# Encoder trunk: the first pair's up-projection weights prepared during the output projection, and a written order for three engines

## The chip, the cores and the metric

The kernel runs on one core of one Trainium2 chip. The metric is the device time of one launch in microseconds (us), as the median of the runs. Engines are named as in the profile: PE is TensorE's matmul, DVE is VectorE, ACT is ScalarE, POOL is GpSimd, and SP issues the DMAs.

## The reference

Two layers, each a mixing part and a gated MLP, on 1024 tokens of 1024 channels, all in float32:

```python
for l in range(DEPTH):
    h = _rmsnorm(x, norm1_g[l])
    ...
    x = x + mix @ w_out[l]

    h2 = _rmsnorm(x, norm2_g[l])
    up = _dwconv3(h2 @ ffn_w_up[l], ffn_conv_w[l])
    gate, val = jnp.split(up, 2, axis=-1)
    x = x + (jax.nn.silu(gate) * val) @ ffn_w_down[l]
```

`ffn_w_up` has 1024 rows and 5632 columns: 22 tiles of 128 columns for the gate and 22 for the value.

## The kernel before, in words

Every float32 product is made of three matmuls in the type fp32r. An operand is split into a high part (a copy to fp32r, on ACT, line 108) and a low part (operand minus high part, on DVE or POOL, line 119); the product is high·high + high·low + low·high (`block_mm`, line 768).

The up projection is done by a scheme with seven products of blocks instead of eight. The activations are cut into four blocks of channels by tokens, the weights of one tile pair (gate tile f, value tile 22 + f) into `b11`, `b21`, `b12`, `b22`. Sums and differences of blocks are the operands. Of the weights these are 11, 21, 22 and the differences T1 to T4, formed in place one after the other by POOL (`up_prep`, line 745); of the activations 11, 12, 22 and the sums S1 to S4. Each tile f takes seven products of 12 matmuls, 84 in all: 11·11, 12·21, S1·T1, S2·T2, S3·T3, S4·22 and 22·T4.

The stage around the change, in both layers:

- `out_proj(b, 1)` is the second half of the output projection for each of eight token blocks b: five splits of the mixing output (ACT and POOL), 24 matmuls on PE, a residual add on DVE (line 661).
- `norm_a` takes the sum of squares on ACT (line 227), the scale 1/sqrt on POOL (lines 123 and 127) and multiplies on DVE (line 229).
- `norm2_b` transposes on PE (line 679), then makes the activation blocks: a split into 11 and 12 for the first four token blocks and into 22 for the last four. For these last four it also forms S3 and S2 on DVE (lines 695 and 696), and S1 and S4 on POOL (lines 697 and 698), in place in two buffers, H2 (S1, S4) and H3 (S3, S2).
- `norm2_end` splits S1 to S4, 1024 columns at a time, ACT high and DVE (or POOL) low.
- `up_ahead` makes 11·11 and 12·21 of tiles 0 and 1 early, since these need no sums (four products, 48 matmuls). `up_prep` forms and splits the rest of the weights. `up_tile` makes the remaining products. Its copies u1 and p5 go to the buffer H3, which becomes free only when S2 and S3 have been split. S3·T3 is summed onto the PSUM bank of S2·T2, so it begins only when u1 has been copied away (line 797).

Nothing in this stage has an order written by hand: the framework's scheduler sets the order of each engine's queue (only the attention's PE queue is written by hand). Each engine then runs its queue strictly in that order.

The lines of the trace: 768 the products, 679 the transposes, 119 and 108 the splits, 745 the weight differences, 695 to 698 the sums, 796 and 797 the adds and copies of `up_tile`.

Of the kernel before, what the change touches and what calls it, by code (L numbers as in the profile page):

```python
# [43 lines left out]
UPRING = ("E0", "E1", "E2", "E5", "E6", "E7", "E9", "G6", "G7")  # L44
# [11 lines left out]
CWE = ("p", "p")  # L56


class Trunk:
# [640 lines left out]
    def norm2_end(self):  # L700

        r0, r1 = self.raw
        for n, src, where, els in (
            ("S1", r0[:, 0:4], self.xo[1], "vv"),
            ("S2", r1[:, 4:8], ("W1", "W4", "Z0", "Z1"), "vv"),
            ("S3", r1[:, 0:4], ("G0", "G2", "G3", "W2"), "vv"),
            ("S4", r0[:, 4:8], ("W5", "G4", "G1", "G5"), "vp"),
        ):
            if isinstance(where, str):
                t = self.A[n] = self.slot(where, [2, 4, 512], F32R)  # L710
                for k in (0, 2):
                    self.split(t[:, 0, k : k + 2], t[:, 1, k : k + 2], src[:, k : k + 2], "a", els[k // 2])
            else:
                t = self.A[n] = [self.S(w, [2, 512], F32R) for w in where]
                for k in range(2):
                    self.split(t[k], t[2 + k], src[:, 2 * k : 2 * k + 2], "a", els[k])

    def a_op(self, n, k):
# [5 lines left out]
    def up_load(self, L, f):  # L724
        raws = []
        for j, m in enumerate((f, NFF + f)):
# [11 lines left out]

    def up_prep(self, f, raws, B):


        b11, b21, b12, b22 = raws

        def sub(out, a, b):
            self.nc.gpsimd.tensor_tensor(out=out, in0=a, in1=b, op=ALU.subtract)  # L745

        if not B:
            B["11"] = self.up_split(b11, "v")
        sub(b11, b12, b11)
        B["T1"] = self.up_split(b11)  # L750
        sub(b11, b22, b11)
        B["T2"] = self.up_split(b11, "v")
        if "21" not in B:
            B["21"] = self.up_split(b21)
        sub(b12, b22, b12)
        B["T3"] = self.up_split(b12, "v")
        B["22"] = self.up_split(b22)
        sub(b21, b21, b11)
        B["T4"] = self.up_split(b21)
# [13 lines left out]
    def up_ahead(self, f, raws):  # L773

        B = {"11": self.up_split(raws[0], "v"), "21": self.up_split(raws[1], "v")}
        u, c2 = self.acc("pa"), self.acc(("po", "pf")[f])
        self.block_mm(u, "11", B["11"], True, False)
        self.block_mm(c2, "12", B["21"], True, True)
        if f == 0:
# [3 lines left out]
        return B, u, c2, p1  # L783

    def up_tile(self, f, B, ahead=None):
# [160 lines left out]
    def run(self, depth):  # L946
# [6 lines left out]
        for L in range(depth):  # L953
# [61 lines left out]
            for b in range(NB + 2):  # L1015
                if b < NB:
                    self.out_proj(b, 1)
                    nc.sync.dma_start(xout[b], self.x[b])
                if 0 <= b - 1 < NB:
                    xs[b - 1] = self.norm_a(b - 1, self.x[b - 1], g2, ("G1", "G5"))  # L1020
                if 0 <= b - 2 < NB:
                    self.norm2_b(b - 2, xs[b - 2])
                if b - 2 in (5, 6):
                    f = len(ahead)
                    raws[f] = self.up_load(L, f)
                    ahead.append(self.up_ahead(f, raws[f]))
            self.norm2_end()
            B = {0: ahead[0][0], 1: ahead[1][0]}
            self.up_prep(0, raws[0], B[0])
            for f in range(NFF):  # L1030
                if f + 1 < NFF:
                    if f + 1 >= 2:
                        raws[f + 1], B[f + 1] = self.up_load(L, f + 1), {}
                    self.up_prep(f + 1, raws.pop(f + 1), B[f + 1])
                self.up_tile(f, B.pop(f), ahead[f][1:] if f < 2 else None)
# [65 lines left out]
```

## Time and profile before

| what | value |
|---|---|
| median of three runs | 2300.79 us (2300.1 to 2304.73) |
| profiled execution, its own time | 2304.89 us |
| its span | 2303.1 us |
| PE busy | 2222.9 us (97%) |
| DVE, ACT, POOL busy | 1657.6, 1121.1, 1287.6 us |

The profiled execution is one run; its span is the time from its first to its last instruction, 1.8 us less than its own time. Times in the trace count from the start of the span. The second half of the output projection of layer 0 ends on PE at about 490 us, that of layer 1 at about 1632 us.

### The profile page before, as it was taken

How to read it: one execution, taken by the hardware profiler on the slowest of the kernel's cores; microseconds unless marked ns; L12 is line 12 of the kernel's file. 1: busy time of each engine (PE TensorE's matmuls, PEld its weight loads, DVE VectorE, ACT ScalarE, POOL GpSimd, SP SyncE). 2: the span in 40 equal slices, each digit the busy share in tenths (PEclk: the TensorE clock that was granted, in tenths of full speed). 3: DMA queues.
4: the chain of work that ended last, by engine and by line, in shares of the span. 5: the costliest groups of instructions: out<-in, count | busy, mean ns of one | idle time of the engine just before them, and what ended most of it. 6: DMA issues, size and time to landing. Idle time of an engine off the chain costs nothing.

```text
span 2303.1 us, 29303 instructions
## 1 busy us (share of the span) xinstructions
PE 2222.9 (97%) x10564; PEld 1840.9 (80%) x10564; DVE 1657.6 (72%) x2123; ACT 1121.1 (49%) x2009; POOL 1287.6 (56%) x1133
## 2 busy tenths in 40 slices
PE   7999999989999999799999999999899999988998
PEld 6887887868888888588878878878688888876887
DVE  5468887276777777988645688862767777779885
ACT  4246776354544444443242467754545444444431
POOL 5463335685555554776454533356765555556761
PEclk9999999999999999899999999999899999999999
DMA  5000003222232325843230000041223333357431
GB/s 183 23 28 10 10 10 95 98 83 87 92 115 92 115 92 175 304 156 106 67 122 6 28 10 10 10 163 48 74 87 101 110 105 105 105 190 268 152 96 74
DMA packets 166852, 218.97 MB, mean 95 GB/s; under 512 B 11799, under 2 KB 117811, under 8 KB 166707
## 3 DMA queue, kind: packets, MB, share of 16 engines
q1 hardware_dynamic: 166706, 217.10, 28.3%
q8 instruction: 83, 1.36, 0.2%
q14 instruction: 63, 0.51, 0.1%
HBM read 159.92 MB, written 57.15 MB: 94 GB/s over the span
## 4 chain that ended last, share of the span: by engine, by line
PE 89%; DVE 4%; POOL 2%; DMA 2%; ACT 1%; issue 1%; SPq 0%; DVEq 0%; POOLq 0%; ACTq 0%
PE pa L768 20%; PE big L920 10%; PE pf L768 9%; PE pf L266 5%; PE po L768 5%; PE pa L536 5%; PE pa L920 3%; PE pa L134 3%; PE pa L133 3%; PE big L520 3%; PE big L519 3%; PE pa L132 3%; PE po L548 2%; PE po L549 2%; PE pf L920 2%; PE po L920 2%
## 5 line engine op out<-in xcount | busy, mean ns | idle before, releaser
L528 POOL TENSOR_SCALAR H<-H,rv 128x1024 f32<-128x1024 f32 x128 | 144.8, 1131 | 272.2 <-DVE rv L527 272.2
L119 POOL TENSOR_TENSOR E<-E,E 128x512 fp32r<-128x512 f32 (+1 forms) x123 | 167.6, 1364 | 172.7 <-ACT E L108 172.2
L108 ACT ACTIVATE E<-E 128x512 fp32r<-128x512 f32 (+1 forms) x227 | 141.6, 629 | 182.0 <-POOL E L745 69.3
L768 PE MATMUL pa<-H,E 128*128 128x512 f32 x840 | 210.8, 395 | 12.3 <-DVE H L796 12.3
L541 DVE TENSOR_TENSOR E<-pa,E 128x512 fp32r<-128x512 f32 x256 | 173.4, 688 | 49.6 <-ACT E L540 48.2
L768 PEld LDWEIGHTS pa<-H,E 128*128 128x128 f32 x840 | 160.0, 191 | 46.7 <-DVE H L796 13.2
L540 ACT ACTIVATE E<-pa 128x512 fp32r<-128x512 f32 x256 | 152.9, 597 | 90.4 <-PE pa L536 89.2
L536 PEld LDWEIGHTS pa<-ident,H 128*128 128x128 f32 x1024 | 128.0, 141 | 42.8 <-issue 5.1
L536 PE MATMUL pa<-ident,H 128*128 128x128 f32 x1024 | 154.9, 274 | 6.6 <-DVE E L541 6.6
L522 DVE TENSOR_REDUCE nm<-big 128x1 f32<-128x1024 f32 x128 | 155.7, 1216 | 6.7 <-PE big L520 6.6
L353 DVE SCALAR_TENSOR_TENSOR big<-H,cst,big 128x1023 f32<-128x1023 f32 x44 | 56.6, 1287 | 143.8 <-ACT big L352 143.8
L797 ACT ACTIVATE H<-pa 128x512 f32<-128x512 f32 x128 | 76.0, 594 | 164.0 <-PE pa L768 148.0
L525 ACT ACTIVATE H<-big,nm 128x1024 f32<-128x1024 f32 x128 | 142.4, 1112 | 17.7 <-DVE nm L522 17.6
L119 DVE TENSOR_TENSOR E<-E,E 128x512 fp32r<-128x512 f32 (+1 forms) x109 | 117.9, 1084 | 24.1 <-ACT E L108 24.1
L266 PE MATMUL pf<-H,G 128*128 128x512 f32 x320 | 130.7, 429 | 2.7 <-DVE Z L394 2.7
L768 PE MATMUL pa<-W,E 128*128 128x512 f32 x340 | 119.2, 400 | 12.7 <-ACT W L108 12.7
L108 ACT ACTIVATE G<-E 128x512 fp32r<-128x512 f32 (+2 forms) x126 | 68.6, 556 | 106.1 <-PE pa L133 21.0
L745 POOL TENSOR_TENSOR E<-E 128x512 f32<-128x512 f32 x66 | 103.1, 1563 | 4.4
L768 PE MATMUL po<-H,E 128*128 128x512 f32 x408 | 104.6, 389 | 0.0
L548 PE MATMUL po<-E,E 128*128 128x512 f32 x256 | 101.5, 396 | 2.1 <-DVE E L564 2.1
L108 ACT ACTIVATE G<-H 128x512 fp32r<-128x512 f32 (+1 forms) x94 | 58.5, 649 | 90.7 <-PE big L920 43.7
L549 PE MATMUL po<-E,E 128*128 128x512 f32 x256 | 101.3, 396 | 0.0
(430 smaller groups left out, 6554.1 us busy)
## 6 DMA issues: line engine op xcount, KB each, us to landing
E<-in_ffn_w_up_dram SPq DMA_DIRECT2D x66, 512.0 KB
gdram<-H SPq DMA_DIRECT2D x66, 512.0 KB
H<-gdram SPq DMA_DIRECT2D x66, 512.0 KB
out_dram<-H SPq DMA_DIRECT2D x32, 512.0 KB
E<-in_w_in_dram SPq DMA_DIRECT2D x30, 512.0 KB
H<-out_dram SPq DMA_DIRECT2D x24, 512.0 KB
H<-in_ffn_w_down_dram SPq DMA_DIRECT2D x24, 512.0 KB
W<-in_ffn_w_up_dram SPq DMA_DIRECT2D x22, 512.0 KB
```

Source lines behind the costliest of these rows:

```text
L108: nc.scalar.activation(out, in_, AF.Copy)
L119: e.tensor_tensor(out=l, in0=src, in1=h.bitcast(F32), op=ALU.subtract)
L266: mm(acc, a[:, k, :], b, start=k + j == 0, stop=k == KC - 1 and j == 2)
L522: nc.vector.tensor_reduce(out=nm, in_=S, op=ALU.max, axis=AX.X, negate=True)
L528: nc.gpsimd.tensor_scalar(out=p, in0=p, scalar1=rv, scalar2=1.0, op0=ALU.mult, op1=ALU.mult)
L536: nc.tensor.transpose(pt[:, r * P : (r + 1) * P], pu[:, r, kc * P : (kc + 1) * P], self.ident)
L540: nc.scalar.activation(hl[:, 0, :], pt, AF.Copy)
L541: nc.vector.tensor_tensor(out=hl[:, 1, :], in0=pt, in1=hl[:, 0, :].bitcast(F32), op=ALU.subtract)
L548: self.nc.tensor.matmul(O, v, hl[:, 0, :], start=kc == 0, stop=False)
L549: self.nc.tensor.matmul(O, v, hl[:, 1, :], start=False, stop=kc == 7)
L768: mm(out, w, x, start=first and k + j == 0, stop=k == 3 and j == 2, skip_group_check=True,)
L920: nc.tensor.matmul(o, p, r, start=n + q == 0 and (m % 2 == 1 or m == 0), stop=n == len(ops) - 1 and q == 2, skip_group_check=True,)
```

## The change

Three things are changed. The weights of tile 0 and half of those of tile 1 are loaded in the program at block 2, and tile 0's 11, 21 and T1 are split, and all its differences formed, at block 4, during the output projection. After the last block of the output projection DVE, POOL and ACT follow the order in which the program is written (`manual_schedule`), up to the end of the preparation of tile 1; in it S2 is split before S1 and S3, and S4 later, with both low parts on DVE. In `up_tile` the first two tiles do S2·T2 before S1·T1. PE's order is still the scheduler's.

```diff
+MANUAL = {mybir.EngineType.DVE, mybir.EngineType.Pool, mybir.EngineType.Activation}
...
-    def norm2_end(self):
+    def norm2_end(self, names):
...
         for n, src, where, els in (
+            ("S2", r1[:, 4:8], ("W1", "W4", "Z0", "Z1"), "vv"),
             ("S1", r0[:, 0:4], self.xo[1], "vv"),
-            ("S2", r1[:, 4:8], ("W1", "W4", "Z0", "Z1"), "vv"),
             ("S3", r1[:, 0:4], ("G0", "G2", "G3", "W2"), "vv"),
-            ("S4", r0[:, 4:8], ("W5", "G4", "G1", "G5"), "vp"),
+            ("S4", r0[:, 4:8], ("W5", "G4", "G1", "G5"), "vv"),
...
+        for n in steps:
+            t = n.upper()
+            if t in subs and t not in self.formed.setdefault(f, set()):
+                p, q = subs[t]
+                self.formed[f].add(t)
+                self.nc.gpsimd.tensor_tensor(out=of[t], in0=p, in1=q, op=ALU.subtract)
+            if n == t:
+                early = f < 2 and n in ("11", "21")
+                B[n] = self.up_split(of[n], "v" if early or n in ("11", "T2", "T3") else "p")
...
-        self.block_mm(c5, "S1", B["T1"], True, False)
-        cp(p5, c5)
+        if not ahead:
+            self.block_mm(c5, "S1", B["T1"], True, False)
+            cp(p5, c5)
         self.block_mm(u, "S2", B["T2"], False, False)
         cp(u1, u)
+        if ahead:
+            self.block_mm(c5, "S1", B["T1"], True, False)
+            cp(p5, c5)
...
+            for b in range(NB):
+                self.norm2_step(b, xs, g2, xout)
+                if b == 2:
+                    raws[0], raws[1] = self.up_load(L, 0), self.up_load(L, 1, (0,))
+                elif b == 4:
+                    self.up_prep(0, raws[0], ("11", "21", "T1", "t2", "t3", "t4"))
+            raws[1] += self.up_load(L, 1, (1,))
+            with self.tc.manual_schedule(engines=MANUAL):
+                xs[7] = self.norm_a(7, self.x[7], g2, ("G1", "G5"))
+                ahead.append(self.up_ahead(0, self.B[0]))
+                self.up_prep(1, raws[1], ("11", "21"))
+                self.norm2_b(6, xs[6])
+                ahead[0] = self.up_ahead_copy(0, *ahead[0])
+                self.up_prep(0, raws[0], ("T2",))
+                self.norm2_b(7, xs[7])
+                self.up_prep(0, raws[0], ("T3",))
+                ahead.append(self.up_ahead(1, self.B[1]))
+                ahead[1] = self.up_ahead_copy(1, *ahead[1])
+                self.norm2_end(("S2", "S1", "S3"))
+                self.up_prep(0, raws[0], ("22",))
+                self.up_prep(1, raws[1], ("t1",))
+                self.up_prep(0, raws[0], ("T4",))
+                self.up_prep(1, raws[1], ("T1", "T2"))
+                self.norm2_end(("S4",))
+                self.up_prep(1, raws[1], ("T3", "22", "T4"))
```

A step name in small letters (t2) only forms the difference; in capitals it also splits it. Lines of the changed kernel are 1 to 18 higher than those before.

On POOL, from the scale of the last block's norm (msx, rsx: the scale's two steps; H2 the buffer of S1 and S4; E3, E8, W3 weights), there stood before:

```order
L745 TENSOR_TENSOR E3_966_4867<-E3_966_4867 128x512
L123 TENSOR_SCALAR msx_975_4908<-ss_974_4906 128x1
L745 TENSOR_TENSOR E8_978_4928<-W3_979_4930,E8_978_4928 128x512
L127 TENSOR_TENSOR rsx_976_4910<-msx_975_4908,mhalf_71 128x1
L697 TENSOR_TENSOR H2_903_4408<-H3_904_4409,H2_903_4408 128x4x128
L698 TENSOR_TENSOR H2_903_4408<-H2_903_4408,H3_904_4409 128x4x128
L119 TENSOR_TENSOR G7_1002_5025<-E3_966_4867,G7_1002_5025 128x512
L745 TENSOR_TENSOR W3_979_4930<-W3_979_4930 128x512
L119 TENSOR_TENSOR E0_1003_5029<-E8_978_4928,E0_1003_5029 128x512
```

and now:

```order
L124 TENSOR_SCALAR msx_975_4893<-ss_974_4891 128x1
L128 TENSOR_TENSOR rsx_976_4895<-msx_975_4893,mhalf_71 128x1
L698 TENSOR_TENSOR H2_903_4408<-H3_904_4409,H2_903_4408 128x4x128
L699 TENSOR_TENSOR H2_903_4408<-H2_903_4408,H3_904_4409 128x4x128
...
L120 TENSOR_TENSOR G7_997_5016<-E4_926_4561,G7_997_5016 128x512
L763 TENSOR_TENSOR E8_927_4563<-W3_972_4886,E8_927_4563 128x512
L120 TENSOR_TENSOR E5_998_5020<-E3_925_4559,E5_998_5020 128x512
```

The scale now stands ahead of the weight differences, and three pairs of sums (the first shown, two more where the dots are) ahead of the weights' low parts.

On DVE, from the last block's S2 on (Z0, Z1 low parts of S2; H5 of S1; G3, W2 of S3; H3 the buffer of S2 and S3), there stood before:

```order
L696 TENSOR_TENSOR H3_904_4409<-big_984_4965,H3_904_4409 128x4x128
L119 TENSOR_TENSOR G3_992_4995<-H3_904_4409,G0_990_4993 128x1024
L119 TENSOR_TENSOR W2_993_4996<-H3_904_4409,G2_991_4994 128x1024
L119 TENSOR_TENSOR Z0_988_4987<-H3_904_4409,W1_986_4985 128x1024
L119 TENSOR_TENSOR Z1_989_4988<-H3_904_4409,W4_987_4986 128x1024
L119 TENSOR_TENSOR E1_1004_5033<-E8_978_4928,E1_1004_5033 128x512
L119 TENSOR_TENSOR H5_985_4980<-H2_903_4408,H5_985_4980 128x1024
L796 TENSOR_TENSOR H3_1008_5047<-po_971_4878,W0_972_4903 128x512
```

and now:

```order
L697 TENSOR_TENSOR H3_904_4409<-big_984_4950,H3_904_4409 128x4x128
L120 TENSOR_TENSOR G6_985_4965<-E4_926_4561,G6_985_4965 128x512
L120 TENSOR_TENSOR Z0_990_4997<-H3_904_4409,W1_988_4995 128x1024
L120 TENSOR_TENSOR Z1_991_4998<-H3_904_4409,W4_989_4996 128x1024
L120 TENSOR_TENSOR H5_992_5003<-H2_903_4408,H5_992_5003 128x1024 x2
L120 TENSOR_TENSOR G3_995_5010<-H3_904_4409,G0_993_5008 128x1024
L120 TENSOR_TENSOR W2_996_5011<-H3_904_4409,G2_994_5009 128x1024
L805 TENSOR_TENSOR H3_1008_5050<-po_978_4899,W0_982_4945 128x512
```

S2 now comes first, then S1, then S3; one weight split (T3 of tile 0) stands ahead of them.

## Rows read from the trace of the kernel before

**Rows 1.** Waits of PE, whole span: us in total, times, longest us.

```profile
PE pa L768 <- ACT W L108: 12.7, 2, 6.3
PE pa L768 <- DVE Z L119: 7.2, 2, 3.6
```

**Rows 2.** PE in order of time, layer 0: start, us, instructions, [idle before].

```profile
490.26 1.04 PE L679 MATMUL big<-ident,G 128*128 128x128 f32 x8
...
501.15 3.34 PE L768 MATMUL pf<-H,E 128*128 128x512 f32 x12
510.81 0.80 PE L768 MATMUL pa<-W,E 128*128 128x512 f32 x1 [6.33 <-ACT W L108]
515.21 0.80 PE L768 MATMUL pa<-Z,E 128*128 128x512 f32 x1 [3.60 <-DVE Z L119]
...
525.68 1.75 PE L768 MATMUL pa<-G,E 128*128 128x512 f32 x7
```

**Rows 3.** PE in order of time, layer 1.

```profile
1632.04 1.03 PE L679 MATMUL big<-ident,G 128*128 128x128 f32 x8
...
1656.97 0.79 PE L768 MATMUL pa<-Z,E 128*128 128x512 f32 x1 [3.61 <-DVE Z L119]
...
1667.97 1.75 PE L768 MATMUL pa<-G,E 128*128 128x512 f32 x7
```

**Rows 4.** Stretches: busy us of each engine, then granted clock, DMA share, GB/s.

```profile
440.00:490.26 50.26, 50.26 (x244) 41.95 (x242) 26.34 (x30) 29.00 (x68) 35.47 (x55) 1.00 0.18 74
510.80:519.40 8.60, 4.99 (x11) 3.62 (x12) 8.60 (x5) 5.30 (x6) 8.60 (x5) 0.50 0.00 0
1656.90:1662.80 5.90, 5.83 (x14) 4.58 (x15) 5.90 (x4) 0.96 (x2) 5.90 (x3) 0.50 0.21 58
939.60:946.00 6.40, 5.20 (x11) 3.65 (x12) 6.40 (x8) 0.00 (x0) 1.64 (x1) 0.50 0.76 271
1536.40:1542.00 5.60, 5.56 (x24) 4.62 (x25) 3.71 (x2) 2.22 (x4) 4.13 (x3) 1.00 0.32 93
```

**Rows 5.** ACT in order of time, layer 0: last sum of squares, a copy u1.

```profile
492.20 1.06 ACT L227 ACTIVATE G<-H 128x1024 f32<-128x1024 f32 x1 [0.27 <-DVE H L661]
...
525.37 0.60 ACT L797 ACTIVATE H<-pa 128x512 f32<-128x512 f32 x1 [1.79 <-DVE G L119]
```

**Rows 6.** POOL in order of time, layer 0.

```profile
495.44 0.51 POOL L123 TENSOR_SCALAR msx<-ss 128x1 f32<-128x1 f32 x1
496.03 1.30 POOL L745 TENSOR_TENSOR E<-W,E 128x512 f32<-128x512 f32 x1
497.28 0.56 POOL L127 TENSOR_TENSOR rsx<-msx,mhalf 128x1 f32<-128x1 f32 x1
...
509.61 2.25 POOL L697 TENSOR_TENSOR H<-H,H 128x512 f32<-128x512 f32 x1
```

**Rows 7.** DVE in order of time, layer 0.

```profile
497.87 2.31 DVE L229 SCALAR_TENSOR_TENSOR G<-H,rsx,E 128x1024 f32<-128x1024 f32 x1 [1.97 <-POOL rsx L127]
500.88 1.00 DVE L119 TENSOR_TENSOR E<-E,E 128x512 fp32r<-128x512 f32 x1 [0.70 <-ACT E L108]
501.80 0.68 DVE L119 TENSOR_TENSOR H<-big,H 128x512 fp32r<-128x512 f32 x1
508.38 2.35 DVE L119 TENSOR_TENSOR G<-H,G 128x1024 fp32r<-128x1024 f32 x1 [0.40 <-ACT G L108]
512.87 4.51 DVE L119 TENSOR_TENSOR Z<-H,W 128x1024 fp32r<-128x1024 f32 x2
522.93 1.21 DVE L119 TENSOR_TENSOR H<-H,H 128x1024 fp32r<-128x1024 f32 x1
```

**Rows 8.** The chain that ended last, in order of time, layer 0: one product.

```profile
541.94 2.72 PE pa L768 x12
```

**Rows 9.** PE in order of time: two waits in other stages.

```profile
939.61 0.80 PE L920 MATMUL pa<-G,G 128*128 128x512 f32 x1 [3.73 <-POOL G L119]
1536.44 0.73 PE L266 MATMUL pf<-H,G 128*128 128x512 f32 x2 [1.83 <-DVE Z L394]
```

More of the change, by code (lines that the diff above doesn't have):

```diff
@@ L43 @@
 D_SUM = "vvvv"
-UPRING = ("E0", "E1", "E2", "E5", "E6", "E7", "E9", "G6", "G7")
+UPRING = ("E0", "E1", "E2", "E6", "E7", "E9", "G6", "G7", "E5")
 GK = "W0"
@@ L716, in norm2_end, with norm2_step @@
                     self.split(t[k], t[2 + k], src[:, 2 * k : 2 * k + 2], "a", els[k])
+    def norm2_step(self, b, xs, g, xout):
+        self.out_proj(b, 1)
+        self.nc.sync.dma_start(xout[b], self.x[b])
+        if b >= 1:
+            xs[b - 1] = self.norm_a(b - 1, self.x[b - 1], g, ("G1", "G5"))
+        if b >= 2:
+            self.norm2_b(b - 2, xs[b - 2])
     def a_op(self, n, k):
@@ L722, in a_op, with up_load @@
         return t[:, 0, k, :], t[:, 1, k, :]
-    def up_load(self, L, f):
+    def up_load(self, L, f, which=(0, 1)):
         raws = []
-        for j, m in enumerate((f, NFF + f)):
+        for j in which:
+            m = f + j * NFF
             v = self.i["ffn_w_up"][L][:, m * P : (m + 1) * P].rearrange("(k p) c -> p k c", p=P)
@@ L737, in up_split, with up_prep @@
         return t
-    def up_prep(self, f, raws, B):
+    def up_prep(self, f, raws, steps=("11", "T1", "T2", "21", "T3", "22", "T4")):
         b11, b21, b12, b22 = raws
[L744 to L759, printed above, removed]
+        B = self.B.setdefault(f, {})
+        of = {"11": b11, "T1": b11, "T2": b11, "21": b21, "T3": b12, "22": b22, "T4": b21}
+        subs = {"T1": (b12, b11), "T2": (b22, b11), "T3": (b22, b12), "T4": (b21, b11)}
+        for n in steps:
[7 more added lines that the diff above has]
+                B[n] = self.up_split(of[n], "v" if early or n in ("11", "T2", "T3") else "p")
     def block_mm(self, out, a, B, first, last):
@@ L778, in up_ahead, with up_ahead_copy @@
         self.block_mm(c2, "12", B["21"], True, True)
+        return u, c2
+    def up_ahead_copy(self, f, u, c2):
         if f == 0:
@@ L782, in up_ahead @@
         self.nc.scalar.activation(p1, u, AF.Copy)
-        return B, u, c2, p1
+        return u, c2, p1
     def up_tile(self, f, B, ahead=None):
@@ L1014, in run @@
             ahead, raws, self.tmp = [], {}, [None, None]
[L1015 to L1026, printed above, removed]
@@ L1027, in run @@
-            self.norm2_end()
-            B = {0: ahead[0][0], 1: ahead[1][0]}
-            self.up_prep(0, raws[0], B[0])
-            for f in range(NFF):
[L1031 to L1035, printed above, removed]
+            self.B, self.formed = {}, {}
+            for b in range(NB):
[4 more added lines that the diff above has]
+                    self.up_prep(0, raws[0], ("11", "21", "T1", "t2", "t3", "t4"))
@@ L1036, in run @@
+            for f in range(NFF):
+                if f > 0 and f + 1 < NFF:
+                    raws[f + 1] = self.up_load(L, f + 1)
+                    self.up_prep(f + 1, raws.pop(f + 1))
+                self.up_tile(f, self.B.pop(f), ahead[f] if f < 2 else None)
             self.alloc_x(self.xreg)
```

5 lines of the change are left out of this document (3 added, 2 removed).

## Prediction, made before the changed kernel was run

> **What bounds the kernel now.** PE is busy for 97% of the span, so time can be gained only where PE waits or runs at a low clock. I read PE's waits first, then PE in order of time around the largest of them, then the granted clock of the stretches, and last the queues of POOL, DVE and ACT to see what PE waits for. Two entries of PE's waits are to be seen: 12.7 us for ACT's high parts of S2 (W) and 7.2 us for DVE's low parts (Z), each in two pieces, one per layer [rows 1]. In layer 0 they stand behind the four products made ahead: the last of these begins at 501.15, and the first product with a sum, S2·T2, gets its first matmul at 510.81 and its second at 515.21 [rows 2]. Layer 1 is the same [rows 3]. After the wait PE has the lower of its two clock levels: 0.50 of 2.4 GHz from 510.8 to 519.4 and from 1656.9 to 1662.8 [rows 4].
>
> What ends the wait is a chain through the second norm of the last token block. ACT's sum of squares starts at 492.20 and takes 1.06 us, so its sum is there at 493.3 [rows 5]. POOL gets to it only at 495.44, and puts another weight difference between the two steps of the scale, which is ready at 497.28 + 0.56 = 497.84 [rows 6]. DVE then multiplies, PE transposes, DVE makes S3 and S2 and splits S3 (from 508.38) before S2 (from 512.87) [rows 7]. PE needs S2 first.
>
> **The change part by part**, in layer 0, on the clock of the trace of before.
>
> Moved into the output projection: tile 0's remaining differences. Two of its four differences and two low parts of it on POOL stood there before; now it is four differences and one low part. By the price of one difference, 1.30 us [rows 6], POOL gets some 1.3 to 2.6 us more in a stretch of 50.26 us in which it is busy for 35.47 us and PE without a gap [rows 4]. I cost this at nothing: POOL's 14.8 idle us hide it. If that cover were gone, each us of it would come late as low parts of the mixing output, for which PE waits one to one. The weights' transfers are no condition: SP's queue has them in the same places as before, and the fourth of them (W3) is needed later than before.
>
> Scale of the last norm: POOL takes its two steps at once, 0.51 + 0.56 us from 493.3 [rows 5, 6], with the small pauses between them 494.2 instead of 497.84. This gains 3.6 us.
>
> DVE's queue from there, in the written order. The multiply: 2.31 us, as in the row of before, since POOL again begins a sum at that moment [rows 7]: 496.5. Two weight splits of 512 columns for tile 1; the row shows 1.00 us beside some POOL work, full overlap would make it nearer 1.8, I take 1.4 each: 499.3. Block 6, three instructions from PSUM, 0.68 us each and one starting every 0.65 us: 2.0 us, 501.3. T2's low part, 0.6: 501.9. Block 7, again 2.0: 503.9. T3's low part, 1.0: 504.9, while ACT makes S2's first high part (1.06 us for 1024 columns). Then six splits of 1024 columns: S2 twice, S1 twice, S3 twice. Their price is what the sum turns on. The rows show 2.35 us and 4.51 us for two while POOL is busy, but 1.21 us (one every 1.13) when it is idle [rows 7]. Both ends: 6.8 us alone, 13.5 us if each meets a POOL instruction. POOL's queue has about four to meet them (the rest of the last sums, 22's low part, a difference for tile 1, T4's low part). I take four at 2.25 and two at 1.13, 11.3 us: 516.2.
>
> A rule of the Trainium skill bears on this price. The page "SBUF — State Buffer", section "Who interferes with whom", says that a DVE instruction with two SBUF inputs and a GpSimd instruction that reads SBUF exclude each other, whichever starts first, for the whole instruction. The trace agrees in the two prices above; taken alone the rule puts the whole of a POOL instruction ahead of each of the six splits, the 13.5 us end, where my sum from the queue has 11.3.
>
> u1 and S3·T3: H3 is free for u1 when S3 has been split, at 516.2; the copy takes 0.60 us [rows 5]; S3·T3 begins at about 517.0 instead of 525.68 [rows 2], 8.7 us earlier. But by 525.68 PE had done 13 matmuls more (four products ahead, S2·T2 of both tiles, S1·T1 and one; now four, S2·T2 and S1·T1 of tile 0). They still have to be done: 13 × 0.227 us (12 in 2.72 us [rows 8]) = 2.9. Gain 5.8 us. Layer 1 starts 1141.78 us later (1632.04 against 490.26) and had its S3·T3 at 1667.97 [rows 3]: 1667.97 − 1658.8 = 9.2, less 2.9, gain 6.3. Together 12.1 us. The low clock of before lies inside these differences.
>
> The new waits and the clock. PE's products ahead end at 503.9, S2·T2 gets its first low part at 504.9 + 2.25 = 507.2 and the second 2.25 later, S1·T1 ends near 513.7, and S3·T3 waits until 517.0: two waits of about 3.3 us with one under 1 us between. A wait of 3.73 us elsewhere is followed by a stretch at 0.50, one of 1.83 us by a stretch at 1.00 [rows 4, 9]; mine are nearer the first. A slow stretch behind the first wait costs nothing, since DVE's chain sets the time there; behind the second it costs half of 6.4 us, 3.2 us per layer. Bounds 0 and 6.4 us for both; I take a third, 2.1 us.
>
> The rest, S4's low parts on DVE, the new order of the weight buffers and some matmuls placed otherwise in the down projection, I cost at 0, give or take 2 us.
>
> Sum: 12.1 − 2.1 = 10.0 us. Against the profiled execution's own 2304.89 that is 2294.9; it lies 4.1 us above the median, and the same gain from 2300.79 gives **2290.8 us**.
>
> **The rivals.**
>
> More is hidden than I think: POOL's instructions fall where DVE works from PSUM, the six splits run at 1.13 us and the multiply at half its price. S3·T3 then starts near 511.5, 11.3 and 11.8 us gained, and no wait is long enough to slow the clock: about 23 us, 2278. For it: DVE's instructions from PSUM cost 0.68 beside a busy POOL [rows 7]. Against it: the written order gives POOL its low parts exactly when ACT has finished the large ones.
>
> Less is gained, since DVE and POOL meet at every one of the six splits. S3·T3 starts at 519.2: 12.1 − 4.4 − 2.1 = 5.6 us, 2295.2; with the slow clock in full behind the longer wait, 12.1 − 4.4 − 6.4 = 1.3 us, 2299.5. For it: the rows from 508 to 517, where every split met one [rows 7]. The rule on the shared port from the page "SBUF — State Buffer", section "Who interferes with whom", speaks for this case.
>
> Slower: POOL's last S1 sum holds up DVE. DVE's order is now written, so S3's low parts stand behind S1's, and S1 needs POOL's last sum. In before it ends at 509.61 + 2.25 = 511.86 [rows 6], where nothing stood behind it. If it comes no earlier, ACT's high part ends at 512.9, four low parts at 2.25 follow, u1 is copied at 522.7: nothing gained in layer 0, 0.5 us in layer 1, and the wait of six us or more slows the clock behind it by 3.2 us per layer: about 6 us slower, 2307. It decides from an end of the S1 sum near 511.9 on. Against it: in before some 5.6 us of weight work stands between the scale and that sum on POOL, which is behind it now, so I expect it at about 506.
>
> **How the numbers follow.** My forecast 0.63 (own range 2285 to 2296), more hidden 0.10, less gained 0.20, slower 0.07. Of the third case I put 0.12 below 2296.2 and 0.08 above it. About 0.2%, 4.6 us, is what a measurement of this kernel tells from no change. Faster 0.63 + 0.10 + 0.12 = 0.85, same 0.08, slower 0.07. The range takes in the forecast and the third case and leaves out most of the two others: 2283 to 2299.
>
> **What would show it.** Right: the scale of block 7 within 1.5 us of its sum of squares; the two waits of PE for S2 fallen from 9.9 us per layer to 2 to 4.5, and a new wait of 2 to 4.5 us ahead of S3·T3, ended by ACT's copy; the output projection's stretch still without a gap on PE. Wrong: gaps on PE during the output projection, a wait for S1, or a product that waits for a weight of tile 1 or 2.

## The result, and the profile after

The changed kernel takes 2288.36 us (median of five runs, 2281.68 to 2294.03), the kernel before 2300.79 us beside it (five runs, 2299.01 to 2305.08): a ratio of 0.994, 95% interval 0.9916 to 0.9964. Run again beside other kernels it took 2288.44 us against 2303.05, ratio 0.9937 (0.9923 to 0.995). The forecast was 2290.8 us, range 2283 to 2299.

The profiled execution of the change has its own time equal to the median; its span is 2286.6 us.

PE's waits over the whole span, of the change (us in total, times, longest):

```profile
PE pa L775 <- DVE H L805: 14.3, 2, 7.2
...
PE pa L775 <- ACT H L806: 5.9, 2, 3.5
PE pa L933 <- ACT G L109: 4.5, 2, 2.2
...
PE pa L775 <- DVE Z L120: 3.7, 3, 1.7
...
PE pa L775 <- ACT W L109: 0.2, 1, 0.2
```

and two entries of the same view of the kernel before, which the prediction did not cost (it used one wait of the second for the clock [rows 9]):

```profile
PE pa L768 <- DVE H L796: 12.3, 2, 6.9
...
PE pa L920 <- POOL G L119: 7.4, 2, 3.7
```

The 12.7 us for S2's high parts [rows 1] are 0.2 us now, the 7.2 us for its low parts 3.7. New is the wait for ACT's copy u1 (H, line 806), 5.9 us. Outside the stage the wait before the last tile's last product has grown from 12.3 to 14.3 us, and the 7.4 us at the start of the down projection, for POOL, are gone; 4.5 us for ACT (line 933) stand there now.

PE of the change in order of time, layer 0, and S3·T3 of layer 1:

```profile
489.14 1.03 PE L680 MATMUL big<-ident,G 128*128 128x128 f32 x8
...
505.21 0.50 PE L775 MATMUL pa<-Z,E 128*128 128x512 f32 x1 [1.65 <-DVE Z L120]
...
507.45 0.50 PE L775 MATMUL pa<-Z,E 128*128 128x512 f32 x1 [0.35 <-DVE Z L120]
...
514.86 3.35 PE L775 MATMUL pa<-G,G 128*128 128x512 f32 x7 [3.47 <-ACT H L806]
...
924.92 5.49 PE L775 MATMUL pa<-H,E 128*128 128x512 f32 x12 [7.17 <-DVE H L805]
...
1648.76 1.89 PE L775 MATMUL pa<-G,G 128*128 128x512 f32 x7 [2.39 <-ACT H L806]
```

S3·T3 begins 25.7 us behind the transposes of 489.14; before it was 525.68 − 490.26 = 35.4 us [rows 2]. In layer 1 it is 25.7 us too, before 1667.97 − 1632.04 = 35.9 [rows 3]. What released it, on ACT, POOL and DVE of the change in order of time:

```profile
491.65 0.19 ACT L228 ACTIVATION_READ_ACCUMULATOR G<-H 128x1 f32 x1
...
514.21 0.60 ACT L806 ACTIVATE H<-pa 128x512 f32<-128x512 f32 x1 [5.15 <-DVE W L120]
```

```profile
486.30 0.55 POOL L128 TENSOR_TENSOR rsx<-msx,mhalf 128x1 f32<-128x1 f32 x1
...
491.93 0.19 POOL L124 TENSOR_SCALAR msx<-ss 128x1 f32<-128x1 f32 x1 [1.61 <-ACT G L228]
492.21 0.55 POOL L128 TENSOR_TENSOR rsx<-msx,mhalf 128x1 f32<-128x1 f32 x1
...
502.36 1.72 POOL L698 TENSOR_TENSOR H<-H,H 128x512 f32<-128x512 f32 x1
504.04 2.27 POOL L699 TENSOR_TENSOR H<-H,H 128x512 f32<-128x512 f32 x1
```

```profile
489.34 0.69 DVE L662 TENSOR_TENSOR H<-po,H 128x512 f32<-128x512 f32 x1 [0.15 <-PE po L135]
...
492.79 1.28 DVE L230 SCALAR_TENSOR_TENSOR G<-H,rsx,E 128x1024 f32<-128x1024 f32 x1
493.99 3.48 DVE L120 TENSOR_TENSOR E<-E,E 128x512 fp32r<-128x512 f32 x2
...
503.04 4.36 DVE L120 TENSOR_TENSOR Z<-H,W 128x1024 fp32r<-128x1024 f32 x2
507.31 2.35 DVE L120 TENSOR_TENSOR H<-H,H 128x1024 fp32r<-128x1024 f32 x2
509.58 2.31 DVE L120 TENSOR_TENSOR G<-H,G 128x1024 fp32r<-128x1024 f32 x1
511.81 2.28 DVE L120 TENSOR_TENSOR W<-H,G 128x1024 fp32r<-128x1024 f32 x1
```

The scale (second line of L128) is ready at 492.76, 0.9 us behind the end of the sum of squares (491.84); the six large splits run from 503.04 to 514.09; the copy u1 follows at once.

Where the time went, from PE in order of time in the two profiles. The "two-tile stage" runs from the end of the output projection's last matmul to the end of the first two tiles' 168 matmuls (all of them are in the rows; the end is taken where the next matmul starts); the "tail" runs from the start of the last tile's last product, behind its wait, to the end of the down projection.

| stretch, us (layer 0, layer 1) | before | change | gained |
|---|---|---|---|
| up to the end of the output projection | 490.4, 478.0 | 489.3, 477.0 | 2.1 |
| two-tile stage | 54.1, 54.6 | 50.2, 47.5 | 11.0 |
| the other tiles | 378.2, 378.2 | 378.2, 378.2 | 0.0 |
| wait before the last product | 5.4, 6.9 | 7.2, 7.2 | −2.0 |
| tail | 226.0, 225.0 | 221.3, 223.9 | 5.9 |

The sum, 17.0, is what PE's last matmul comes earlier (2296.9 to 2279.9; the span fell by 16.5). The first and third line are stretches whose work is the same in both; the third took the same time to 0.1 us, the first varied by several us from run to run, all of it ahead of the output projection's second half. What the change touches is the second line, as forecast, and the last two. Of the kernel before there is one trace, 4.1 us above its median, so these two profiles alone don't show how much of the tail's gain is the change's and how much that execution's.

### The profile page after: what moved, and what is told of

It reads as the page before. It is cut to its first block, busy times and chain, and to the rows that moved or that the text cites. A ratio compares the mean times of both kernels' runs of the same rounds, so it can differ in the third digit from the quotient of the medians.

```text
span 2286.6 us, 29313 instructions
## 1 busy us (share of the span) xinstructions
PE 2217.6 (97%) x10564; PEld 1839.6 (80%) x10564; DVE 1646.3 (72%) x2125; ACT 1121.4 (49%) x2009; POOL 1278.5 (56%) x1131
## 4 chain that ended last, share of the span: by engine, by line
PE 90%; DVE 4%; DMA 2%; ACT 2%; issue 1%; POOL 1%; SPq 0%; DVEq 0%; ACTq 0%; POOLq 0%
PE pa L775 20%; PE big L933 10%; PE pf L775 9%; PE po L775 5%; PE pf L267 5%; PE pa L537 5%; PE pa L933 3%; PE pa L135 3%; PE pa L134 3%; PE pa L133 3%; PE big L520 3%; PE big L521 3%; PE po L549 2%; PE po L550 2%; PE po L933 2%; PE pf L933 2%
## 5 line engine op out<-in xcount | busy, mean ns | idle before, releaser
L775 PE MATMUL pa<-H,E 128*128 128x512 f32 x864 | 216.7, 396 | 14.3 <-DVE H L805 14.3
L542 DVE TENSOR_TENSOR E<-pa,E 128x512 fp32r<-128x512 f32 x256 | 173.4, 688 | 49.3 <-ACT E L541 47.7
L775 PEld LDWEIGHTS pa<-H,E 128*128 128x128 f32 x864 | 164.6, 191 | 49.5 <-DVE H L805 15.2
L120 DVE TENSOR_TENSOR E<-E,E 128x512 fp32r<-128x512 f32 (+1 forms) x107 | 107.9, 1018 | 17.5 <-ACT E L109 17.5
L943 DVE TENSOR_TENSOR H<-big,H 128x1024 f32<-128x1024 f32 x64 | 77.3, 1215 | 31.7 <-PE big L933 31.7
```

The costliest lines, as they stand in the source:

```text
L120: e.tensor_tensor(out=l, in0=src, in1=h.bitcast(F32), op=ALU.subtract)
L542: nc.vector.tensor_tensor(out=hl[:, 1, :], in0=pt, in1=hl[:, 0, :].bitcast(F32), op=ALU.subtract)
L775: mm(out, w, x, start=first and k + j == 0, stop=k == 3 and j == 2, skip_group_check=True,)
```

## The experiments

One table first; each run's two-tile stage and tail are read from the PE rows of its profiled execution as above (before: stage 54.1, 54.6, tail 226.0, 225.0).

| run | median us | ratio to before (95%) | stage, layers 0, 1 | tail, layers 0, 1 |
|---|---|---|---|---|
| change again | 2288.44 | 0.9937 (0.9923 to 0.995) | 47.5, 49.1 | 225.4, 221.2 |
| no written order | 2298.78 | 0.9985 (0.9976 to 0.9993) | 54.2, 53.3 | 223.7, 221.3 |
| order only | 2294.13 | 0.9956 (0.9942 to 0.997) | 51.8, 51.8 | 224.0, 221.0 |
| S1 first | 2288.27 | 0.9939 (0.9926 to 0.9951) | 49.1, 47.7 | 221.4, 224.2 |
| scale late | 2290.82 | 0.995 (0.9937 to 0.9962) | 52.7, 51.4 | 221.2, 224.0 |
| u1 elsewhere | 2286.39 | 0.9931 (0.9918 to 0.9945) | 45.9, 45.9 | 225.4, 225.2 |
| POOL quiet | 2284.88 | 0.9925 (0.9906 to 0.9944) | 46.4, 46.4 | 221.2, 223.9 |
| both | 2278.9 | 0.9898 (0.9885 to 0.9911) | 45.0, 45.0 | 225.0, 221.0 |
| six more on POOL | 2299.52 | 0.999 (0.9982 to 0.9998) | 52.5, 51.5 | 223.8, 224.0 |
| two more on POOL | 2291.36 | 0.9948 (0.9935 to 0.9962) | 51.6, 51.8 | 221.2, 221.2 |
| S4 on both | 2287.39 | 0.9937 (0.9924 to 0.9951) | 50.0, 49.1 | 221.2, 223.9 |
| ring only | 2300.42 | 0.9987 (0.9979 to 0.9996) | 54.3, 54.3 | 223.0, 222.6 |

### Which half of the change: the weights or the order

Without the written order (the early weights stay):

```diff
-            with self.tc.manual_schedule(engines=MANUAL):
+            if True:
```

> The change without its written order: tile 0's weights and differences are still prepared in the output projection, but the queues of DVE, POOL and ACT behind it are again the scheduler's. In them POOL has a low part of 22 ahead of the last norm's scale and a difference of tile 1 between its two steps. Theory (the chain from the sum of squares over the scale and DVE's splits to S2 and S3 sets the time, one to one): the scale comes 2 to 3 us later than with the change, the waits of PE between the products ahead and S3*T3 grow from 5.5 us to 8 to 12 us per layer, and the kernel is slower than the change by 5 to 10 us: 2293 to 2299 us, 2 to 8 us faster than before. Rival (the early weights alone bring the gain, the order is only for safety): within 2 us of the change's 2288. Rival (the gain lies in other stages, by another order of the last tile and the down projection): the waits here grow, but the time stays at 2286 to 2291.

2298.78 us: of the stage's gain 1.2 us are left. The scheduler put other weight work into the queues of POOL and DVE. POOL, then DVE, then PE, of this run in order of time:

```profile
491.54 1.74 POOL L120 TENSOR_TENSOR G<-E,G 128x512 fp32r<-128x512 f32 x1
495.70 0.19 POOL L124 TENSOR_SCALAR msx<-ss 128x1 f32<-128x1 f32 x1 [2.42 <-ACT G L228]
495.97 1.29 POOL L763 TENSOR_TENSOR E<-W,E 128x512 f32<-128x512 f32 x1
```

```profile
490.34 3.49 DVE L120 TENSOR_TENSOR E<-E,E 128x512 fp32r<-128x512 f32 x2
493.75 0.68 DVE L662 TENSOR_TENSOR H<-po,H 128x512 f32<-128x512 f32 x1
```

```profile
506.62 0.53 PE L775 MATMUL pa<-W,E 128*128 128x512 f32 x1 [3.01 <-ACT W L109]
512.33 0.80 PE L775 MATMUL pa<-W,E 128*128 128x512 f32 x1 [5.17 <-ACT E L109]
```

The weight difference between the two steps of the scale, which stood there before [rows 6], stands there still: it is one of tile 1, and the early work on tile 0 did not move it. The low part ahead of both steps cost nothing, since POOL then waits 2.42 us for the sum of squares. That sum is late because of DVE: the last residual add (L662), which it needs, stands behind two weight splits and begins 4.2 us behind the output projection, with the change 0.05. PE waits 8.7 us again in this layer: 3.01 for S2's high part, 5.17 for the high part of a weight of tile 1, whose difference POOL formed only at 509.38, and 0.55 for S1's. The other half alone, the order without the early differences:

```diff
-                    self.up_prep(0, raws[0], ("11", "21", "T1", "t2", "t3", "t4"))
+                    self.up_prep(0, raws[0], ("11", "21"))
...
                 xs[7] = self.norm_a(7, self.x[7], g2, ("G1", "G5"))
+                self.up_prep(0, raws[0], ("T1", "t2", "t3", "t4"))
```

> The written order without the early differences: in the output projection only 11 and 21 of tile 0 are split; T1 to T4 are formed, and T1 split, by POOL behind the last norm's scale and ahead of the last sums, some 6.5 us of its work there, of which it had 4.8 us idle with the change. The scale stays early. Theory (the order brings most of the gain, the early weights keep POOL free for the last sums): POOL's last S1 sum ends 2 to 4 us later than the change's, S1's and S3's splits and u1 follow, the stage to the end of the first two tiles takes 50 to 53 us in place of 47.5 to 50.2, and the time is 2 to 6 us above the change's 2288.4: 2290 to 2295. Rival (the order alone does it): within 1 us of the change. Rival (the case that the prediction priced as slower: the last S1 sum holds up DVE's written order altogether): the stage 54 us or more in both layers, 2297 to 2303.

2294.13 us, 5.0 us of the stage's gain. POOL's last S1 sum ended 19.8 us behind the output projection, with the change 14.8 (504.08 − 489.30); S3·T3 came 2.8 us later than the change's. DVE of this run:

```profile
503.03 1.11 DVE L120 TENSOR_TENSOR E<-E,E 128x512 fp32r<-128x512 f32 x1 [1.30 <-ACT E L109]
...
507.18 4.30 DVE L120 TENSOR_TENSOR Z<-H,W 128x1024 fp32r<-128x1024 f32 x2
511.53 3.32 DVE L120 TENSOR_TENSOR H<-H,H 128x1024 fp32r<-128x1024 f32 x2
```

The late sum is not what held S3·T3 up: S1's splits (511.53) follow S2's without a pause. S2's splits themselves begin 2.8 us later, 16.6 us behind the output projection (507.18 − 490.62) and with the change 13.7, since the multiply met a difference on POOL (2.30 us in place of 1.28) and T2's low part waited 1.30 us for a high part whose difference POOL had formed only then. So the halves alone bring 1.2 (weights) and 5.0 us (order), both together 11.0 (12.1 in the profile of the second run): they need each other.

### The chain to S3·T3

Two differences back between the steps of the scale:

```diff
+        if mid:
+            mid()
         self.nc.gpsimd.tensor_tensor(out=r, in0=ms, in1=self.mhalf[:, 0:width], op=ALU.pow)
...
-                    self.up_prep(0, raws[0], ("11", "21", "T1", "t2", "t3", "t4"))
+                    self.up_prep(0, raws[0], ("11", "21", "T1", "t2"))
...
-                xs[7] = self.norm_a(7, self.x[7], g2, ("G1", "G5"))
+                late = lambda: self.up_prep(0, raws[0], ("t3", "t4"))
+                xs[7] = self.norm_a(7, self.x[7], g2, ("G1", "G5"), late)
```

> The change with two of tile 0's differences (T3, T4) put back between the two steps of the last norm's scale on POOL, some 2.6 us of POOL's time there; they are no longer formed in the output projection. Theory (each us by which the scale is late moves the whole chain, one to one): the scale is ready 2.6 us later, S3*T3 starts 2.2 to 2.8 us later behind the first transposes, 4.4 to 5.6 us slower than the change in two layers, 2292.5 to 2294. Rival (DVE's queue has slack between the multiply and the splits, or waits for POOL's sums anyway): less than 1 us per layer, 2288 to 2290. Rival (the longer wait before S2 drops PE's clock for longer): 4 us and more per layer, 2296 and above.

The stage grew to 52.7 and 51.4 us; against stages of the change with the same low-clock stretch behind S3·T3 (50.2 and 49.1) that is 2.5 and 2.3 us for 2.5 us on POOL, one to one. The median rose by only 2.4 us, below what was expected, with a spread of 5 us: the stage shows it more sharply than the time does.

S1 ahead of S2 again, in `norm2_end` and in the first two tiles:

```diff
-            ("S2", r1[:, 4:8], ("W1", "W4", "Z0", "Z1"), "vv"),
             ("S1", r0[:, 0:4], self.xo[1], "vv"),
+            ("S2", r1[:, 4:8], ("W1", "W4", "Z0", "Z1"), "vv"),
...
-        if not ahead:
-            self.block_mm(c5, "S1", B["T1"], True, False)
-            cp(p5, c5)
+        self.block_mm(c5, "S1", B["T1"], True, False)
+        cp(p5, c5)
         self.block_mm(u, "S2", B["T2"], False, False)
         cp(u1, u)
-        if ahead:
-            self.block_mm(c5, "S1", B["T1"], True, False)
-            cp(p5, c5)
```

> The change with S1 ahead of S2 again, in the order of the splits and of the first two tiles' products; all else is kept. Theory (only the time at which all six large splits are done sets S3*T3; which of S1 and S2 comes first moves the first wait alone, and PE has to wait for the last splits in any case): the first wait is for S1's parts, later by some 2 us since POOL's last S1 sum ends 2 us after DVE's S2 (504.0 against 501.9), the wait further on is that much shorter, and the kernel is within 3 us of the change, 2286 to 2292 us. Rival (S2 first is the point of the order): the first wait grows to 5 us and more, PE's clock falls behind it, 4 to 8 us slower per launch: 2292 to 2297 us.

2288.27 us, nothing lost. DVE of this run:

```profile
505.18 2.36 DVE L120 TENSOR_TENSOR H<-H,H 128x1024 fp32r<-128x1024 f32 x2 [2.24 <-ACT H L109]
507.46 2.35 DVE L120 TENSOR_TENSOR Z<-H,W 128x1024 fp32r<-128x1024 f32 x2
509.73 1.22 DVE L120 TENSOR_TENSOR G<-H,G 128x1024 fp32r<-128x1024 f32 x1
510.87 2.31 DVE L120 TENSOR_TENSOR W<-H,G 128x1024 fp32r<-128x1024 f32 x1
```

DVE starts 2.1 us later, but by then POOL has ended its sums: five of the six splits take about 1.2 us and one 2.31, and the sixth ends at 513.2 where the change's ended at 514.1. So S2 first is not what gains. The earlier end of the six splits gained nothing here either: in ACT's order p5 and a weight's high part now stand ahead of u1, u1 began at 514.87, and S3·T3 at 516.03, 1.2 us later behind the transposes than with the change (layer 0).

The new wait, attacked from two sides. First u1 and p5 in the half of H3 that S2 filled, so that they need not wait for S3's split:

```diff
-            self.tmp[f] = self.slot(self.hreg[0][1 - f], [4, 1024])
+            self.tmp[f] = (
+                self.raw[1].rearrange("p (a b) t -> p a (b t)", a=4)
+                if f == 0
+                else self.slot(self.hreg[0][1 - f], [4, 1024])
+            )
```

> The change with one thing more: tile 0's copies u1 and p5 go into the half of H3 that S2 filled, as a view of that tile, so that they wait for the split of S2 alone and not for that of S3. Theory (the new wait before S3*T3 is for H3 by the copy u1): that wait of 3.5 us goes; S3*T3 starts when S3's first low part is there, some 2.9 us earlier (at the end of DVE's fifth large split and not 0.75 us after the sixth), and two smaller waits of under 1 us for the sixth take its place. 1.5 to 2.5 us per layer gained, and up to 3 us more per layer if PE's clock no longer falls there: 2279 to 2286 us. Rival (PE waits for the splits themselves, and H3 is named only because it came last): no change, 2286 to 2290, with the wait put down to DVE's G.

PE of this run in order of time, and a stretch of it (busy us of PE, PE's weight loads, DVE, ACT, POOL; clock, DMA share, GB/s):

```profile
510.50 1.66 PE L775 MATMUL pa<-G,G 128*128 128x512 f32 x6 [0.34 <-DVE G L120]
```

```profile
500.00:520.00 20.00, 16.52 (x67) 11.81 (x66) 16.74 (x13) 12.21 (x17) 15.30 (x9) 1.00 0.18 53
```

The wait is gone, and the clock stays at 1.00; the stage is 45.9 us in both layers, 1.6 below the change's shortest. The time, 2286.39, is just above what was expected; in the profiled execution, which is the median, the tail came out at its longest in both layers.

Second, POOL without work beside S3's splits. The run with this and the run with both edits:

```diff
                 self.norm2_b(6, xs[6])
+                self.up_prep(1, raws[1], ("t1",))
...
                 self.up_prep(0, raws[0], ("22",))
-                self.up_prep(1, raws[1], ("t1",))
...
-                B[n] = self.up_split(of[n], "v" if early or n in ("11", "T2", "T3") else "p")
+                B[n] = self.up_split(of[n], "v" if early or n in ("11", "T2", "T3") or (f < 1 and n in ("22", "T4")) or (f == 1 and n == "T1") else "p")
```

> The change with POOL left without work while S3 is split: the low parts of 22 and T4 of tile 0 and of T1 of tile 1 are made by DVE, behind S3 in its order, and tile 1's first difference is formed by POOL before the last sums. Theory (a POOL instruction on SBUF beside each split makes it 2.3 us where it takes 1.13 alone): the last two to three large splits take 1.1 to 1.3 us each, u1 is copied 2 to 2.5 us earlier, the wait before S3*T3 falls from 3.5 to about 1.2 us, the stage to the end of the first two tiles is 1.5 to 2.5 us shorter per layer than the change's 50.2 and 47.5 (up to 3 more where the clock no longer falls): 2279 to 2286 us. Rival (the splits wait for ACT's high parts or for each other, not for POOL): the splits start as late as now, less than 0.5 us per layer. Rival (DVE becomes the bound, since it has three low parts more): a new wait of S4*22 or 22*T4 for DVE, no gain.

DVE, then POOL, of the run with POOL quiet:

```profile
507.68 3.33 DVE L120 TENSOR_TENSOR H<-H,H 128x1024 fp32r<-128x1024 f32 x2
510.94 1.21 DVE L120 TENSOR_TENSOR G<-H,G 128x1024 fp32r<-128x1024 f32 x1
512.07 1.21 DVE L120 TENSOR_TENSOR W<-H,G 128x1024 fp32r<-128x1024 f32 x1
```

```profile
506.52 2.27 POOL L699 TENSOR_TENSOR H<-H,H 128x512 f32<-128x512 f32 x1
```

S3's two splits take 1.21 us each in place of 2.31 and 2.28, with nothing changed in them but POOL's silence. S3·T3 came 1.1 us earlier and not 2 to 2.5, since the difference that POOL now forms earlier put its last sums back (that of S1 ends at 506.6, with the change at 504.1): the very last, S4's at 506.52, ran beside S1's first split, and the two S1 splits took 3.33 us in place of 2.35. The wait before S3·T3 was 1.3 us, and no low clock followed.

> POOL quiet during S3 and u1 in the half of H3 that S2 filled, both. Theory: the two act on the same wait, so they don't add: with u1 elsewhere the wait before S3*T3 is gone already (stage 45.9 us in both layers), and what is left are waits of 0.3 to 0.6 us for the low parts of S3 and for T4, which now come earlier: 0.5 to 1.5 us per layer less than 45.9, thus 44.4 to 45.4. The time then hangs on the last tile and the down projection, which took 228.4 to 232.7 us in the runs so far: 2278 to 2287 us. Rival (they add): 43.5 us or less. Rival (DVE's further low parts are late): 46 us or more.

45.0 us in both layers, 2278.9 us: faster than the change's 2288.44 beside it, the two intervals apart. This version beats both kernels. The stage explains 6.5 of these 9.5 us; the rest was not traced.

### What the output projection can hide

Six, then two, more differences formed on POOL at block 4:

```diff
                     self.up_prep(0, raws[0], ("11", "21", "T1", "t2", "t3", "t4"))
+                    for n in range(6):
+                        o = raws[0][(0, 2, 0, 2, 0, 0)[n]]
+                        nc.gpsimd.tensor_tensor(out=o, in0=raws[0][3], in1=o, op=ALU.subtract)
```

> The change with six more differences of 1.30 us on POOL in the output projection (each forms a difference again, twice over, so that the values stay the same): 7.8 us in a stretch in which POOL had 14.8 idle us before the change, less the 1.3 to 2.6 us that the change took. Theory (the idle time of POOL hides it): the second half of the output projection stays at 47.6 us, the stage behind it at 50 and 47.5 us, the time at 2286 to 2291. Rival (the idle time lies in pieces between the blocks' low parts, and each piece has an owner): the low parts of the mixing output or the scale come late by 3 to 8 us per layer, PE has gaps in the output projection or before the transposes, 2295 to 2304 us.

> As the run with six more differences on POOL in the output projection, but with two, 2.6 us. With six the output projection's second half took 50.9 us where it takes 47.6, and the stage behind it 51 to 52 us. Theory (POOL's idle time there is cover only as far as it lies ahead of the last blocks' low parts; the change left a few us of it): with two more the output projection stays at 47.6 us and the stage at 47 to 51 us, the time within 2 us of the change's 2288.4. Rival (the change used the cover up): each further us counts, 1.5 to 2.6 us per layer, 2291 to 2294.

With six, the second half of the output projection took 51.1 us instead of 47.8 (the expectations, with 50.9 and 47.6, leave out its first matmul). Of the 3.3 us 1.31 are a gap on PE for POOL's low part, and 1.8 are eight matmuls of tile 0's first product, which PE's order now has there. The stage, though it has these no more, was longer too: 2299.52 us, 11.1 of the change's 14.6 us are gone (the profile is that of the slowest of twelve runs, 2306.15 us). With two the output projection kept its 47.8 us, but the stage took 51.6 and 51.8 us, 1.4 to 1.6 more than the change's stage with the same low-clock stretch. The time, 2291.36 us, alone would not tell this run from the change: the two intervals overlap. POOL, then DVE, of that run:

```profile
490.06 0.55 POOL L128 TENSOR_TENSOR rsx<-msx,mhalf 128x1 f32<-128x1 f32 x1
```

```profile
490.64 2.30 DVE L230 SCALAR_TENSOR_TENSOR G<-H,rsx,E 128x1024 f32<-128x1024 f32 x1 [0.21 <-POOL rsx L128]
492.87 0.68 DVE L662 TENSOR_TENSOR H<-po,H 128x512 f32<-128x512 f32 x1
```

That is the scale of the last but one block: ready at 490.6, by the end of the output projection (490.55); with the change it was ready at 486.85, 2.4 us ahead of it. Its multiply now stands in DVE's way when the last residual add (L662) could begin: 492.87 in place of 489.34 with the change, 2.3 against 0.05 us behind the output projection.

### The rest of the change

S4's second low part back on POOL:

```diff
-            ("S4", r0[:, 4:8], ("W5", "G4", "G1", "G5"), "vv"),
+            ("S4", r0[:, 4:8], ("W5", "G4", "G1", "G5"), "vp"),
```

> The change with the second low part of S4 back on POOL. Theory (S4's low parts lie behind the stage's critical wait and cost nothing on either engine): no product waits for S4, the stage stays at 47 to 50.5 us, the time within 2 us of the change's 2288.4. Rival (POOL's share of S4 falls beside tile 1's low parts and holds up a weight): a new wait of 1 us or more for a weight of tile 1 or 2, 2290 to 2293.

No difference, and no wait for S4: costed at nothing, rightly. The kernel before with the change's ring of weight buffers:

```diff
-UPRING = ("E0", "E1", "E2", "E5", "E6", "E7", "E9", "G6", "G7")
+UPRING = ("E0", "E1", "E2", "E6", "E7", "E9", "G6", "G7", "E5")
```

> The kernel before with one thing of the change alone: the new order of the ring of weight buffers, with E5 last. All else, the scheduler's queues too, is as the scheduler then makes it. It tells apart where the two gains outside the stage come from: with the change the last tile's last product waits 7.16 us in every run, where it waited 5.4 and 6.9, and the stretch from the end of that wait to the end of the down projection took 221.2 to 225.4 us, where it took 226.0 and 225.0. Theory (the ring sets which buffers the last tile and the first down weights find free): 7.16 us here too, and 221 to 225 us per layer behind it; the stage of the second norm stays at 53 to 55 us; 2297 to 2303 us. Rival (the stretch hangs on PE's clock behind the wait, whatever the ring): the stretch takes either value, with the lower ones where the product behind the wait runs at the lower clock throughout. Rival (it was chance in the one profile of before): 5.4 and 6.9 us, 226 and 225 us again.

PE of this run, layer 0:

```profile
928.86 5.49 PE L768 MATMUL pa<-H,E 128*128 128x512 f32 x12 [7.15 <-DVE H L796]
```

The last product waits 7.15 and 7.16 us here too, 2.0 us more than before over both layers, and the tails are 223.0 and 222.6 us, 5.5 less; PE's waits for POOL at the start of the down projection, 7.4 us before, are 0.7. Together 3.5 us; the medians, 2300.42 us against 2302.86, say 2.4, with an interval of 0.9 to 4.8. So nearly all that the change moves outside the stage comes with the ring (and what the scheduler makes of it), as far as one profile of each shows it; how the ring does it was not followed further.

The change once more:

> The change itself, once more beside the other runs. Counted from the end of the output projection to the end of the first two tiles' 168 matmuls, the change took 50.2 us in layer 0 and 47.5 us in layer 1, before 53.8 and 54.1. Theory (the order of the queues is fixed, so the waits repeat and only PE's clock behind the wait before S3*T3 can differ): the same waits within 0.3 us, the stage between 47 and 51 us in each layer, the last tile and the down projection 228.4 and 231.0 us again within 3 us; 2285 to 2291 us. Rival (layer 1's shorter stage is a property of its data or transfers): 50 and 47.5 again in the same order.

The waits in front of S2 repeated to 0.4 us, that before S3·T3 was 2.53 and 2.54 us where it had been 3.47 and 2.39, and the short and the long stage had changed places: 47.5 and 49.1. S3·T3 began 25.7 to 25.8 us behind the transposes in all four stages, so the wait before it is only what a low clock ahead of it leaves over. The tail of layer 0 missed the 3 us, 225.4 where it had been 221.3. (Before, counted in full, the stage took 54.1 and 54.6 us, not 53.8 and 54.1.)

## Why the prediction was right, and where it was not

**The bound and the chain: right.** The waits for S2 and S3·T3 were the place, and S3·T3 moved 9.7 us in layer 0 (35.4 to 25.7), forecast 8.7. Less the 13 matmuls that remain, 2.9 us, that is 6.8; forecast 5.8. In layer 1 it is 7.3, forecast 6.3.

**The scale: right.** Forecast 3.6 us; it comes 3.62 us behind the transposes (492.76 − 489.14), before 7.58 (497.84 − 490.26): 4.0 gained. The 494.2 of the forecast is 0.2 less than its own terms give (493.3 + 0.51 + 0.56); the two steps took 0.19 and 0.55 us.

**DVE's queue: right in the sum.** The multiply got in ahead of POOL's sum, 1.28 us where I took 2.31; the two weight splits met one each, 3.48 us for both where I took 2.8. The six large splits took 11.05 us, forecast 11.3: four met POOL at 2.2 to 2.3 us, two ran alone (2.35 for both). The page "SBUF — State Buffer" of the Trainium skill, section "Who interferes with whom", has it that a DVE instruction with two SBUF inputs contends with a GpSimd instruction that reads SBUF, and that the shared port pair is an exclusive lock. The quiet run agrees, 1.21 us without POOL and 2.3 with it; but the end of 13.5 us that the rule taken alone gave did not come, as POOL had nothing to do from 506.3 to 508.6, when S1's splits began.

**The new waits and the clock: right in kind, one size off.** The wait before S3·T3 stands there, ended by ACT's copy, 3.5 and 2.4 us, forecast 3.3. That for S2's low parts is 2.0 us in two pieces in layer 0 and 1.7 in layer 1, where I had 3.3 and something under 1. The clock I priced at 2.1 us in a range of 0 to 6.4. Stages of the change without a low stretch behind S3·T3 took 47.5 us, one with it (below, 513.50 to 520.50) 50.2: 2.7 us in one layer, none in the other, and 1.6 in the second run.

**Sum of the stage: 11.0 us, forecast 10.0.** Two errors stand against each other in it: S3·T3 came about 2 us earlier over both layers than forecast (14 for 12.1), and about 3 us were lost behind it where I took 2.1. That the sum came out so near is in part luck.

**The moved work "costs nothing": right in the result, wrong in the reason.** The output projection's second half took 47.8 us before and after, and PE had no gap in it. But POOL was busy for 4.0 us more there and not 1.3 to 2.6: 38.96 us (below, 441.30 to 488.90), and before, in the same stretch (busy us of PE, PE's weight loads, DVE, ACT, POOL):

```profile
442.43:490.03 47.60, 47.60 (x232) 39.81 (x231) 26.08 (x30) 28.80 (x68) 34.97 (x54) 1.00 0.19 78
```

And the 14.8 idle us of POOL are not cover as a whole. The idle time lies between the blocks; two more differences already cost 1.4 to 1.6 us per layer, six cost most of the gain. The change uses most of what could be hidden.

**The term that was mis-sized: "the rest, 0 give or take 2 us".** Between the two profiles it measured 3.9 us: −2.0 before the last product and +5.9 in the tail. The ring alone showed 3.5 between profiles. By the medians, less the stage as profiled, it is smaller: 12.4 − 11.0 = 1.4 us in the first set of runs, 14.6 − 12.1 = 2.5 in the second, 2.4 for the ring alone. I had said "the new order of the weight buffers and some matmuls placed otherwise in the down projection"; that was the place, and I didn't look for what waited there, though 7.4 us of PE's waits for POOL stood in the list. The kernel is 2.4 us below the forecast in the first set of runs: 1.0 of it is the stage, 1.4 this term. The profiles differ by more than the medians, 16.5 us against 12.4, since the profiled run of before lies 4.1 us above its median; 2.1 us of the difference lie ahead of the output projection, which the change doesn't touch.

**The rivals.** "More is hidden" came in one part, the multiply at half its price, but not in the splits; "less is gained" did not come, as only four of six splits met POOL. "Slower" needed POOL's last S1 sum after 511.9 on the clock of before; it ended at 504.08, 505.2 on that clock, forecast about 506. Its mechanism did not show in the run with the order alone either: there that sum came 5.0 us later, at 510.4 (510.2 on the clock of before), and S1's splits still followed S2's without a pause. No run with the written order has an end beyond 511.9 on that clock, so what the rival says of it was not put to the test.

## What the runs showed of the hardware

In the runs of the change and its variants the tail took one of three lengths: about 221.2, 223.9 or 225.3 us, even for one and the same program (layer 0 of the change: 221.3, and 225.4 when run again). What differs is where PE's clock is low and a wait for DVE some 17 us behind the tail's start. Stretches of the change (columns as above), first the output projection, then behind S3·T3, then the tail's start and 17.5 us behind it; last the wait:

```profile
441.30:488.90 47.60, 47.60 (x231) 39.79 (x230) 25.70 (x28) 27.56 (x65) 38.96 (x56) 1.00 0.20 78
...
513.50:520.50 7.00, 5.64 (x13) 4.46 (x14) 1.33 (x3) 3.55 (x6) 5.51 (x4) 0.53 0.31 92
...
920.00:930.20 10.20, 5.28 (x12) 3.80 (x12) 10.12 (x9) 2.38 (x3) 10.20 (x8) 0.50 0.72 250
942.42:949.42 7.00, 7.00 (x32) 5.79 (x31) 7.00 (x11) 0.18 (x1) 3.48 (x3) 1.00 0.56 218
```

```profile
941.90 0.94 PE L933 MATMUL pa<-E,E 128*128 128x512 f32 x3 [1.86 <-DVE H L943]
```

and of the second run:

```profile
917.00:923.80 6.80, 3.79 (x9) 3.02 (x10) 6.71 (x7) 1.75 (x2) 6.80 (x6) 0.50 0.54 181
...
937.50:944.50 7.00, 6.19 (x15) 4.88 (x16) 7.00 (x11) 0.00 (x0) 1.90 (x2) 0.51 0.51 195
```

```profile
938.31 1.62 PE L933 MATMUL pa<-E,E 128*128 128x512 f32 x3 [3.91 <-DVE H L943]
```

In the first run the low stretch goes on through the whole last product (5.49 us for 12 matmuls), the wait is 1.86 us, and the stretch from 942.42 is at 1.00. In the second, whose tail starts at 920.00, the low stretch ends earlier, the wait is 3.91 us, and the stretch from 937.50, as far behind the start, is at 0.51. So the run whose last product was slower had the shorter tail by 4 us. Why the clock falls in the one and not in the other, and whether the longer wait comes of it, no run here settles. Differences of this kind stand in every comparison of times above, and those of 2 to 4 us are better made stage by stage.

## What to carry to other kernels

Idle time of a helper engine is cover only in front of the instruction that the next engine waits for; test it with two more instructions before counting on it. Where a scheduler fills an engine's queue, freeing it is not enough: without the written order other weight work stood ahead of the residual add on DVE and between the scale's two steps on POOL. A new wait for a buffer is worth a look at which half of it is really still in use, and a change of a buffer ring is worth a look at every stage that takes the ring's buffers over.
